# One chain of reciprocal roots per attention, dilated attention in three parts, gate rows one step later

## The chip, the cores and the metric

The kernel runs on one core of a Trainium2 chip. A core has a matrix engine (TensorE, PE in the profile; its weight loads are PEld), three engines for elementwise work (VectorE is DVE, ScalarE is ACT, GpSimd is POOL) and SyncE (SP), which issues most DMA transfers. Each engine executes its own instructions in order and waits on semaphores for the others. The metric is the device time of one execution in microseconds (us), which every time below is in. "Granted clock" is the share of full TensorE speed that the throttle granted in a stretch.

## The reference

One decoder layer for 256 tokens of width 2048, in float32. Three token mixers read the same normalised input and are gated, summed and projected; a SwiGLU block of width 5632 follows.

```python
def mixing_sublayer(h, w_in, ...):
    proj = h @ w_in                              # split by columns
    (q_sb, k_sb, v_sb, q_dil, k_dil, v_dil, q_gla, k_gla, v_gla, r_gla, a_gla, gate_cols) = ...
    qa, ka = rms_norm(heads(q_sb), gain), rms_norm(heads(k_sb), gain)     # 6 heads of 128
    o_sb = stick_breaking_attention(qa, ka, v_sb)
    qb, kb = rms_norm(heads(q_dil), gain), rms_norm(heads(k_dil), gain)   # 6 heads of 128
    o_dil = dilated_mixture(qb, kb, v_dil, slopes)
    o_g = gla_chunked(q_gla, k_gla, v_gla, log_a)                         # 4 heads
    o_gla = rms_norm(o_g, gain) * silu(r_gla)
    g = sigmoid(gate_cols.reshape(b, t, 3, d))
    y = g0 * (o_sb @ w_br_sb) + g1 * (o_dil @ w_br_dil) + g2 * (o_gla @ w_br_gla)
    return y @ w_out
# layer: mod = silu(c) @ w_ada + b_ada gives six vectors of 2048: shift1, scale1, gate1, shift2, scale2, gate2
x = x + gate1 * mixing_sublayer(rms_norm(x) * (1 + scale1) + shift1)
x = x + gate2 * swiglu(rms_norm(x) * (1 + scale2) + shift2)
```

`rms_norm` of a head multiplies it by the reciprocal root of the mean of its squares. The dilated mixture runs a softmax attention for each of three groups of two heads, and mixes the groups by the softmax of their log-denominators (lse).

## The kernel before

**Matmuls.** Each float32 weight matmul is done as three with rounded operands (`mm3`, L154 to L156): both operands are held as a high and a low part, and high*high, high*low and low*high are summed in PSUM. `load_weights` brings weights in pieces of 512 KB: a DMA into `raw`, issued from SP; a cast on ACT to `whi` (L148); a subtraction on DVE to `wlo` (L149), called "split" below. There are four buffers each of `whi` and `wlo`. A block is one product of 512 output columns for both halves of the tokens: with all 16 chunks of K it is 96 matmuls of 512 columns. It accumulates in banks named `acc` (four in PSUM); all else uses banks named `misc` (four too).

**Order.** A scheduler orders the instructions on each engine by program order, dependences and priorities. What stands in `prio()` (weight loads, casts, splits and the copies that empty a finished block) is moved ahead by 4000 places; `tc.issue_after(x)` holds an instruction back until x is issued. So small work written between two blocks in the program falls among the matmuls of the next blocks.

**Stages.** After the modulation vectors and the first norm, `proj_block` multiplies by the columns of q, k and v in four groups along K. In the last group come blocks 0 to 4, `stick_breaking()`, `gla()`, blocks 5 to 8, `dilated()`, then two blocks of r (stage "r"), then the gates: `gate_block(0, 0..2)` copies three finished blocks to `A` buffers, and one sigmoid over each of these three is issued later (L914); the gate blocks (1, 0..2) and further follow, with the sigmoid taken straight from PSUM. Behind them are the branch products, w_out, the second norm and the FFN.

**Norms of q and k.** `qk_norm(b, h0, h1, gain)` does one block of projections at a time: squares on ACT with a sum for each head and half of the tokens (L569); `rsqrt` on the 4 to 8 sums, which is one DVE operation, Ln and Exp on ACT (L242 and L243) and four small DVE operations ending with L248; a multiply on DVE for each half of the tokens (L574, up to four heads wide); transposes on PE, four into one bank (L581), and one eviction for each bank on ACT, which applies the gain (L582). Stick-breaking calls it for blocks 0, 1 and 2 (eight sums each), dilated attention for blocks 4 to 7 (24 sums in all).

**Dilated attention.** `dilated()` then multiplies scores for each head (L768, L769) into a bank, adds the bias on DVE, takes the exponential with its sum on ACT, forms lse and its softmax (a Ln, an Exp and small DVE operations, L781 to L792), the coefficients (L795 to L797), scales the probabilities (L806, 18 operations), transposes them (L810), copies them out of PSUM on ACT (L812) and multiplies by v (L813, L814). The result is split into the buffer OD.

**Modulation in the background.** Three modulation vectors (shift2, gate1, scale2) are summed on DVE while the mixers run (L257, L259): a DMA brings 512 KB of `w_ada` into a buffer of the ring `ring["tags"]`, and one DVE operation adds it up. `tick` advances this by `state["rate"]` steps (0.8, then 0.6 at the r blocks, 0.4 in the FFN) for every two chunks of K of a block. The gate vectors are then spread over all partitions by `rows_of`: for each 256 columns a cast and a split into the buffer T6 (L846, L847) and, one step later, two products with a matrix of ones (L850, L851). gate1 goes this way during the branch products, gate2 in the FFN.

Of the kernel before, what the change touches and what calls it, by code (L numbers as in the profile page):

```python
# [10 lines left out]
F32 = mybir.dt.float32  # L11
F32R = mybir.dt.float32r
U8 = mybir.dt.uint8
AF = mybir.ActivationFunctionType
ALU = mybir.AluOpType
AX = mybir.AxisListType

P = 128
T = 256
NT = T // P  # L20
D = 2048
KC = D // P
# [44 lines left out]
def trunk(ctx: ExitStack, tc: tile.TileContext, I, out):  # L67
# [21 lines left out]
    def scr(shape, dtype=F32):  # L89
        return sp.tile(shape, dtype, tag="scr", name=nm("scr"))  # L90
# [4 lines left out]
    def misc_bank(shape):  # L95
        return psm.tile(shape, F32, tag="misc", name=nm("misc"))
# [81 lines left out]
    ident = const.tile([P, P], F32, name="ident")  # L178
    make_identity(nc, ident)
    made = next(i for i in reversed(nc.cur_bb.bb.instructions) if i.engine == mybir.EngineType.Pool)  # L180
    ones = const.tile([P, P], F32, name="ones")
    nc.vector.memset(ones, 1.0)
    ones_r = const.tile([P, P], F32R, name="ones_r")
    nc.vector.tensor_copy(ones_r, ones)
    eps_c = const.tile([P, 2], F32, name="eps_c")
    nc.vector.memset(eps_c[:, 0:1], EPS)
    nc.vector.memset(eps_c[:, 1:2], 1.5)

# [369 lines left out]
    def head2(c):  # L558
        return A[c // 4][:, :, (c % 4) * P : (c % 4 + 1) * P]

    def qk_norm(b, h0, h1, gain):

        n = h1 - h0
        blk = A[b].rearrange("p t (h d) -> p t h d", d=P)
        ss = small([P, NT, n])
        for t in range(NT):
            for h in range(n):
                junk = scr([P, P])
                nc.scalar.activation(junk, blk[:, t, h0 + h, :], AF.Square, accum_out=ss[:, t, h : h + 1])  # L569
        r = rsqrt(ss.rearrange("p t h -> p (t h)"), 1.0 / P, [P, NT * n])  # L570
        r = r.rearrange("p (t h) -> p t h", t=NT)
        for t in range(NT):
            v = blk[:, t, h0:h1, :]
            nc.vector.tensor_tensor(  # L574
                v, v, r[:, t, :].unsqueeze(2).to_broadcast([P, n, P]), op=ALU.mult
            )
        for h in range(h0, h1, 2):
            ps = misc_bank([P, NT, 2, P])
            for t in range(NT):
                for i in range(2):  # L580
                    nc.tensor.transpose(ps[:, t, i, :], blk[:, t, h + i, :], ident)  # L581
            nc.scalar.activation(blk[:, :, h : h + 2, :], ps, AF.Copy, scale=gain(h))  # L582


    W3 = 3 * P
# [2 lines left out]
    def stick_breaking():  # L588
        os_ = [S(f"OS{j}", [P, 2, 2, T], F32R) for j in range(3)]
        hi = [o[:, 0] for o in os_]  # L590
        lo = [o[:, 1] for o in os_]
        qn = lambda h: qg_sb[:, 0:1]
        kn = lambda h: vec[:, ROW_SBK : ROW_SBK + 1]
        qk_norm(0, 0, 4, qn)
        qk_norm(1, 0, 4, lambda h: qn(h) if h < 2 else kn(h))
        qk_norm(2, 0, 4, kn)
        for h in range(N_SB):
            cq, ck, cv = h, N_SB + h, 2 * N_SB + h
            z = misc_bank([P, W3])
            nc.tensor.matmul(z[:, 0:T].rearrange("p (t d) -> p t d", t=NT), head(ck, 0), head2(cq), start=True, stop=True)  # L600
            nc.tensor.matmul(z[:, T:W3], head(ck, 1), head(cq, 1), start=True, stop=True)
            soft = scr([P, W3])
            nc.scalar.activation(soft, z, AF.Abs)
            nc.scalar.activation(soft, soft, AF.Exp, scale=-1.0)
            nc.scalar.activation(soft, soft, AF.Ln, bias=1.0)
            neg = scr([P, W3])
            nc.vector.scalar_tensor_tensor(neg, z, 0.0, soft, op0=ALU.max, op1=ALU.add)
            for d0 in (0, T):
                nc.vector.tensor_mul(neg[:, d0 : d0 + P], neg[:, d0 : d0 + P], causal)
            lb = soft  # L610
            nc.vector.scalar_tensor_tensor(lb, z, 0.0, soft, op0=ALU.min, op1=ALU.subtract)
            cum = misc_bank([P, W3])
            nc.tensor.matmul(cum, low, neg, start=True, stop=False)  # L613
            nc.tensor.matmul(cum[:, P:T], ones, neg[:, T:W3], start=False, stop=True)
            nc.vector.tensor_tensor(lb, lb, cum, op=ALU.subtract)
            w = neg
            nc.scalar.activation(w, lb, AF.Exp)
            for d0 in (0, T):
                nc.vector.tensor_mul(w[:, d0 : d0 + P], w[:, d0 : d0 + P], causal)
            o = misc_bank([P, T])  # L620
            nc.tensor.matmul(o, head(cv, 0), w[:, 0:T], start=True, stop=False)
            nc.tensor.matmul(o[:, P:T], head(cv, 1), w[:, T:W3], start=False, stop=True)
            split_from_psum(hi[h // 2][:, h % 2, :], lo[h // 2][:, h % 2, :], o)
        return hi, lo
# [125 lines left out]
        return og  # L750


    def dilated():
        qn = lambda h: qg_sb[:, 1:2]
        kn = lambda h: vec[:, ROW_DILK : ROW_DILK + 1]
        qk_norm(4, 2, 4, qn)
        qk_norm(5, 0, 4, qn)
        qk_norm(6, 0, 4, kn)
        qk_norm(7, 0, 2, kn)
        prob = [S(f"T{j}", [P, 2, W3]) for j in range(3)]  # L760
        mx = const.tile([P, NT, N_DIL], F32, name="dmax")
        sm = const.tile([P, NT, N_DIL], F32, name="dsum")
# [27 lines left out]
        den = small([P, NT, 2])  # L790
        nc.vector.tensor_add(den, G(lse, 0), G(lse, 1))
        nc.vector.tensor_add(den, den, G(lse, 2))  # L792
        coef = const.tile([P, NT, N_DIL], F32, name="dcoef")
        for g in range(3):
            nc.vector.tensor_mul(G(coef, g), G(sm, g), den)  # L795
# [3 lines left out]
        for j in range(2):  # L799
            o = misc_bank([P, T])  # L800
            for g in range(3):
                h = 2 * g + j
                cv = 30 + h
                p = prob[g][:, j, :]
                for t, (a, b) in enumerate(spans):
                    nc.vector.tensor_scalar(p[:, a:b], p[:, a:b], coef[:, t, h : h + 1], None, op0=ALU.mult)  # L806

                pt = misc_bank([P, W3])
                for i in range(3):
                    nc.tensor.transpose(pt[:, i * P : (i + 1) * P], p[:, i * P : (i + 1) * P], ident)  # L810
                pT = scr([P, W3])
                nc.scalar.copy(pT, pt)  # L812
                nc.tensor.matmul(o, head(cv, 0), pT[:, 0:T], start=g == 0, stop=False)  # L813
                nc.tensor.matmul(o[:, P:T], head(cv, 1), pT[:, T:W3], start=False, stop=g == 2)  # L814
            split_from_psum(oT[:, 0, j, :], oT[:, 1, j, :], o)
# [15 lines left out]
    def rows_of(name, seg, acc):  # L831

        quarters = [a[:, c : c + NB] for a in acc for c in (0, NB)]
        for j, q in enumerate(quarters):
            br = scr([1, NB])
            nc.sync.dma_start(br, I["b_ada"][:, seg * D + j * NB : seg * D + (j + 1) * NB])
            nc.vector.tensor_add(q[0:1, :], q[0:1, :], br)
            yield
        for _ in range(4):
            yield  # L840
        for q in quarters:
            ps = misc_bank([P, NB])
            for c in (slice(0, T), slice(T, NB)):
                hl = S("T6", [P, 2, T], F32R)
                hi, lo = hl[:, 0, :], hl[:, 1, :]
                nc.scalar.copy(hi, q[:, c])  # L846
                nc.vector.tensor_tensor(lo, q[:, c], hi.bitcast(F32), op=ALU.subtract)  # L847
                yield
                with tc.issue_after(state["mm"].ins):
                    nc.tensor.matmul(ps[:, c], ones_r, hi, start=True, stop=False)  # L850
                    nc.tensor.matmul(ps[:, c], ones_r, lo, start=False, stop=True)  # L851
            nc.scalar.copy(q, ps)
            yield
        state[name] = quarters
# [19 lines left out]
    og = gla()  # L874
    for b in range(5, 9):
        proj_block(LAST, b)
    od = dilated()

    state["rate"] = RATE_MID
    ring["tags"] = ("AR0", "AR1", "KC", "KD")  # L880

    rr = []
    for j in range(2):
        pss = [acc_bank() for _ in range(NT)]
        block(pss, h_at, w_in, 0, KC, (13 + j) * NB)
        r = S(f"A{j}", [P, NT, NB])
        with prio():
            for t in range(NT):
                nc.scalar.copy(r[:, t, :], pss[t])
        rr.append(r)  # L890

    gtags = (("A2", "A3", "A4"), ("A7", "A8", "T0"))
    gates = {}

    def gate_block(n, br):
        pss = [acc_bank() for _ in range(NT)]
        c0 = COL_G + br * D + n * NB
        block(pss, h_at, w_in, 0, KC, c0)
        g = S(gtags[n % 2][br], [P, NT, NB])
        with prio():  # L900
            for t in range(NT):
                if n == 0:
                    nc.scalar.copy(g[:, t, :], pss[t])
                else:
                    nc.scalar.activation(g[:, t, :], pss[t], AF.Sigmoid)
        gates[n, br] = g

    for br in range(3):
        gate_block(0, br)


# [264 lines left out]
```

## Time and profile before

| what | value |
|---|---|
| median of three runs | 1629.87 (1628.82 to 1631.06) |
| the profiled execution | 1630.8, of which span 1629.0 |
| granted TensorE clock, mean | 0.998 |
| matmuls | 7346 |
| first scores of stick-breaking (L600) | 276.1 |
| first transposes of dilated attention (L581 for blocks 4 to 7) | 460.7 |
| first products with v of dilated attention (L813) | 503.7 |
| row sums of gate1 and gate2 (L851) | 661.2 to 1289.4 |

The span runs from the first to the last recorded instruction of one execution; the profiled execution's own time adds what lies around it. The times in the last three rows are starts, counted from the span's start, which is also how rows of the timeline are given: start, duration, engine, line, operation, output<-input by buffer names, shapes, and the number of instructions that the row groups; brackets hold the engine's idle time before the row and what ended it. In a list of waits each line gives the instruction that waited, what it waited for, the total, the number of waits and the longest. A row of the windows view gives a stretch, its length, for each engine in the order PE, PEld, DVE, ACT, POOL its busy time with the number of instructions in brackets, then the granted clock, the busy share of DMA, and GB/s.

### The profile page before, as it was taken

The numbers are of one execution on the slowest core, as the hardware profiler recorded it, in microseconds if no ns is written. First come the engines' busy times: TensorE is split into PE (matmuls) and PEld (weight loads), VectorE is DVE, ScalarE is ACT, GpSimd is POOL, SyncE is SP. The second block draws the span as 40 slices with busy tenths as digits, with TensorE's granted clock in tenths as the row PEclk, the third lists the DMA queues.
The fourth block names the chain that finished last, engine by engine and source line by source line (L and its number), as shares of the span: only waits on it lengthen the run. The fifth ranks groups of instructions, "written<-read, shape, count | busy, mean of one in ns | idle before, by whom it ended". The sixth has DMA issues, their size and how long they took to land.

```text
span 1629.0 us, 19997 instructions
## 1 busy us (share of the span) xinstructions
PE 1608.1 (99%) x7346; PEld 1325.8 (81%) x7346; DVE 1121.9 (69%) x1322; ACT 801.5 (49%) x1130; POOL 5.3 (0%) x14
## 2 busy tenths in 40 slices
PE   8999999999999999999999999999999999999998
PEld 7878888788777888788887888888888888888887
DVE  6799996869688787877756566767655555454453
ACT  4654449764775444444446544444444444333332
POOL 1000000000000000000000000000000000000000
PEclk9999999999999999999999999999999999999999
DMA  9999996865777999988766478887666666666663
GB/s 319 339 333 325 329 312 201 287 224 167 230 225 247 308 310 312 306 278 303 258 192 209 147 236 262 273 269 257 211 192 182 191 187 189 192 205 194 205 207 109
DMA packets 194593, 395.94 MB, mean 243 GB/s; under 512 B 12914, under 2 KB 27928, under 8 KB 194496
## 3 DMA queue, kind: packets, MB, share of 16 engines
q1 hardware_dynamic: 194272, 394.67, 74.6%
q8 instruction: 57, 0.93, 0.2%
q14 instruction: 40, 0.33, 0.1%
q0 software_dynamic: 224, 0.01, 0.0%
HBM read 392.53 MB, written 2.10 MB: 242 GB/s over the span
## 4 chain that ended last, share of the span: by engine, by line
PE 88%; DMA 5%; DVE 3%; ACT 2%; issue 1%; SPq 0%; DVEq 0%; ACTq 0%
PE acc L156 28%; PE acc L154 28%; PE acc L155 27%; DMA raw<-w_in 2%; DMA raw<-w_br_gla 1%; ACT whi L148 1%; DMA A<-w_ada 1%; DVE wlo L149 1%; DMA KD<-w_ada 1%; PE misc L701 1%; PE misc L962 1%; DVE ada L259 1%; PE misc L308 0%; DMA raw<-w_ffn_in 0%; PE misc L613 0%
## 5 line engine op out<-in xcount | busy, mean ns | idle before, releaser
L149 DVE TENSOR_TENSOR wlo<-raw,whi 128x1024 fp32r<-128x1024 f32 (+1 forms) x546 | 651.8, 1198 | 431.4 <-ACT whi L148 429.5
L148 ACT CAST whi<-raw 128x1024 fp32r<-128x1024 f32 (+1 forms) x546 | 561.7, 1032 | 706.3 <-PE acc L156 561.8
L155 PE MATMUL acc<-wlo,H 128*128 128x512 f32 x1576 | 616.9, 391 | 1.0 <-DVE wlo L149 1.0
L154 PE MATMUL acc<-whi,H 128*128 128x512 f32 x1576 | 616.2, 392 | 0.5 <-ACT H L416 0.4
L156 PE MATMUL acc<-whi,H 128*128 128x512 f32 x1576 | 616.2, 391 | 0.4 <-DVE H L422 0.4
L156 PEld LDWEIGHTS acc<-whi,H 128*128 128x128 f32 x1576 | 296.4, 188 | 63.3 <-DVE H L422 1.5
L155 PEld LDWEIGHTS acc<-wlo,H 128*128 128x128 f32 x1576 | 296.6, 188 | 61.5 <-DVE wlo L149 1.4
L154 PEld LDWEIGHTS acc<-whi,H 128*128 128x128 f32 x1576 | 296.7, 188 | 61.3 <-ACT H L416 0.9
L155 PE MATMUL acc<-wlo,A 128*128 128x512 f32 x312 | 121.5, 390 | 0.6 <-DVE wlo L149 0.6
L154 PE MATMUL acc<-whi,A 128*128 128x512 f32 x312 | 121.9, 391 | 0.0
L156 PE MATMUL acc<-whi,A 128*128 128x512 f32 x280 | 109.1, 390 | 0.0
L259 DVE SCALAR_TENSOR_TENSOR ada<-AR,csil,ada 128x1024 f32<-128x1024 f32 x59 | 75.2, 1278 | 3.7 <-DMA AR<-w_ada 3.6
L155 PEld LDWEIGHTS acc<-wlo,A 128*128 128x128 f32 x312 | 58.6, 188 | 12.9 <-DVE wlo L149 1.0
L154 PEld LDWEIGHTS acc<-whi,A 128*128 128x128 f32 x312 | 58.6, 188 | 11.9
L156 PEld LDWEIGHTS acc<-whi,A 128*128 128x128 f32 x280 | 52.6, 188 | 11.1
L154 PE MATMUL acc<-whi,T 128*128 128x512 f32 x120 | 46.7, 389 | 0.0
L155 PE MATMUL acc<-wlo,T 128*128 128x512 f32 x120 | 46.7, 389 | 0.0
L156 PE MATMUL acc<-whi,T 128*128 128x512 f32 x120 | 46.7, 389 | 0.0
L156 PE MATMUL acc<-whi,OS 128*128 128x512 f32 x112 | 43.6, 390 | 0.0
L459 ACT COPY A<-acc 128x512 f32<-128x512 f32 x50 | 29.0, 585 | 17.6 <-PE acc L156 16.4
L259 DVE SCALAR_TENSOR_TENSOR ada<-OS,csil,ada 128x1024 f32<-128x1024 f32 (+2 forms) x33 | 35.6, 1078 | 1.1 <-DMA OS<-w_ada 0.9
L461 DVE TENSOR_TENSOR A<-A,acc 128x512 f32<-128x512 f32 x48 | 31.5, 682 | 2.0 <-PE acc L156 1.8
(334 smaller groups left out, 1227.9 us busy)
## 6 DMA issues: line engine op xcount, KB each, us to landing
raw<-w_in SPq DMA_DIRECT2D x205, 512.0 KB, 5.1
raw<-w_ffn_in SPq DMA_DIRECT2D x176, 512.0 KB, 3.9
raw<-w_ffn_out SPq DMA_DIRECT2D x88, 512.0 KB, 4.6
AR<-w_ada SPq DMA_DIRECT2D x79, 512.0 KB, 5.0
raw<-w_out SPq DMA_DIRECT2D x32, 512.0 KB, 4.4
KC<-w_ada SPq DMA_DIRECT2D x30, 512.0 KB, 5.5
KD<-w_ada SPq DMA_DIRECT2D x19, 512.0 KB, 5.6
OS<-w_ada SPq DMA_DIRECT2D x16, 512.0 KB, 6.7
```

What stands on the lines that cost most here:

```text
L148: state["cast"] = nc.scalar.copy(hi[:, :n, :], raw[:, :n, :])
L149: state["split"] = nc.vector.tensor_tensor(lo[:, :n, :], raw[:, :n, :], hi[:, :n, :].bitcast(F32), op=ALU.subtract)
L154: nc.tensor.matmul(ps, lh, rh, start=start, stop=False, skip_group_check=seeded)
L155: nc.tensor.matmul(ps, lh, rl, start=False, stop=False, skip_group_check=seeded)
L156: state["mm"] = nc.tensor.matmul(ps, ll, rh, start=False, stop=stop, skip_group_check=seeded)
L259: nc.vector.scalar_tensor_tensor(acc, raw, c, acc, op0=ALU.mult, op1=ALU.add)
L459: nc.scalar.copy(A[b][:, t, :], pss[t])
L461: nc.vector.tensor_add(A[b][:, t, :], A[b][:, t, :], pss[t])
L701: nc.tensor.matmul(ps[:n, h, L:], at(lhs, h, t)[:, :n], at(rhs, h, t)[:, L:], start=True, stop=True)
L962: nc.tensor.transpose(ps[:, i, :], src[:, i * P : (i + 1) * P], ident)
```

## The change

- **Norms**: `qk_norm(parts)` takes all blocks of an attention at once. It issues all squares, one `rsqrt` over 24 sums, and all multiplies. The transposes and evictions are in the new `qk_turn(parts, behind)`, which holds the transposes back behind an instruction if one is given. Stick-breaking calls the two in a row.
- **Dilated attention**: `qk_norm(dil_parts)` is called after projection block 8, where `dilated()` stood. `dilated()` now holds the transposes, scores and lse; it is called after r block 0, with its transposes behind the last matmul issued. The coefficients and all that follows are the new `mixture()`, called after `gate_block(0, 0)`, its transposes held back in the same way.
- **Ring**: its fourth buffer is OD instead of KD until `mixture()` is called, and KD from then on.
- **Gate rows**: one more step lies between a split and its two products in `rows_of`.
- **Ones**: the float32 tile of ones becomes a view of the rounded one, `ones_r`.

```diff
-    ones = const.tile([P, P], F32, name="ones")
-    nc.vector.memset(ones, 1.0)
+    eps_c = const.tile([P, 3], F32, name="eps_c")
+    nc.vector.memset(eps_c[:, 2:3], 1.0)
     ones_r = const.tile([P, P], F32R, name="ones_r")
-    nc.vector.tensor_copy(ones_r, ones)
-    eps_c = const.tile([P, 2], F32, name="eps_c")
+    nc.vector.tensor_copy(ones_r, eps_c[:, 2:3].to_broadcast([P, P]))
+    ones = ones_r.bitcast(F32)
...
-    def qk_norm(b, h0, h1, gain):
+    def qk_norm(parts):
-        n = h1 - h0
-        blk = A[b].rearrange("p t (h d) -> p t h d", d=P)
+        n = sum(h1 - h0 for _, h0, h1, _ in parts)
         ss = small([P, NT, n])
+        places, o = [], 0
+        for b, h0, h1, _ in parts:
+            for t in range(NT):
+                for h in range(h0, h1):
+                    junk = scr([P, P])
+                    i = o + h - h0
+                    nc.scalar.activation(junk, heads(b)[:, t, h, :], AF.Square, accum_out=ss[:, t, i : i + 1])
+            places.append(slice(o, o + h1 - h0))
+            o += h1 - h0
         r = rsqrt(ss.rearrange("p t h -> p (t h)"), 1.0 / P, [P, NT * n])
...
+        for (b, h0, h1, _), c in zip(parts, places):
+            for t in range(NT):
+                v = heads(b)[:, t, h0:h1, :]
+                nc.vector.tensor_tensor(
+                    v, v, r[:, t, c].unsqueeze(2).to_broadcast([P, h1 - h0, P]), op=ALU.mult
+                )
+
+    def qk_turn(parts, behind=None):
+        for b, h0, h1, gain in parts:
+            for h in range(h0, h1, 2):
+                ps = misc_bank([P, NT, 2, P])
+                for t in range(NT):
+                    for i in range(2):
+                        with tc.issue_after(behind) if behind is not None else nullcontext():
+                            nc.tensor.transpose(ps[:, t, i, :], heads(b)[:, t, h + i, :], ident)
+                nc.scalar.activation(heads(b)[:, :, h : h + 2, :], ps, AF.Copy, scale=gain(h))
...
-        qk_norm(0, 0, 4, qn)
-        qk_norm(1, 0, 4, lambda h: qn(h) if h < 2 else kn(h))
-        qk_norm(2, 0, 4, kn)
+        parts = ((0, 0, 4, qn), (1, 0, 4, lambda h: qn(h) if h < 2 else kn(h)), (2, 0, 4, kn))
+        qk_norm(parts)
+        qk_turn(parts)
...
+    dil_parts = ((4, 2, 4, dil_q), (5, 0, 4, dil_q), (6, 0, 4, dil_k), (7, 0, 2, dil_k))
     def dilated():
-        qk_norm(4, 2, 4, qn)
...
+        qk_turn(dil_parts, state["mm"].ins)
...
+        return prob, sm, lse, den, spans
+
+    def mixture(prob, sm, lse, den, spans):
+        G = lambda x, g: x[:, :, 2 * g : 2 * g + 2]
         coef = const.tile([P, NT, N_DIL], F32, name="dcoef")
...
-                    nc.tensor.transpose(pt[:, i * P : (i + 1) * P], p[:, i * P : (i + 1) * P], ident)
+                    with tc.issue_after(state["mm"].ins):
+                        nc.tensor.transpose(pt[:, i * P : (i + 1) * P], p[:, i * P : (i + 1) * P], ident)
... rows_of:
                 nc.vector.tensor_tensor(lo, q[:, c], hi.bitcast(F32), op=ALU.subtract)
                 yield
+                yield
                 with tc.issue_after(state["mm"].ins):
...
     for b in range(5, 9):
         proj_block(LAST, b)
-    od = dilated()
+    qk_norm(dil_parts)
     state["rate"] = RATE_MID
-    ring["tags"] = ("AR0", "AR1", "KC", "KD")
+    ring["tags"] = ("AR0", "AR1", "KC", "OD")
... for j in range(2):  (blocks of r)
         rr.append(r)
+        if j == 0:
+            groups = dilated()
...
-    for br in range(3):
+    gate_block(0, 0)
+    ring["tags"] = ("AR0", "AR1", "KC", "KD")
+    od = mixture(*groups)
+    for br in range(1, 3):
         gate_block(0, br)
```

More of the change, by code (lines that the diff above doesn't have):

```diff
@@ L559, in head2, with heads @@
         return A[c // 4][:, :, (c % 4) * P : (c % 4 + 1) * P]
-    def qk_norm(b, h0, h1, gain):
-        n = h1 - h0
-        blk = A[b].rearrange("p t (h d) -> p t h d", d=P)
+    def heads(b):
+        return A[b].rearrange("p t (h d) -> p t h d", d=P)
+    def qk_norm(parts):
+        n = sum(h1 - h0 for _, h0, h1, _ in parts)
         ss = small([P, NT, n])
[L566 to L569, printed above, removed]
+        places, o = [], 0
[7 more added lines that the diff above has]
+            o += h1 - h0
@@ L570, in qk_norm @@
         r = rsqrt(ss.rearrange("p t h -> p (t h)"), 1.0 / P, [P, NT * n])
         r = r.rearrange("p (t h) -> p t h", t=NT)
[L572 to L578, printed above, removed]
-            for t in range(NT):
-                for i in range(2):
-                    nc.tensor.transpose(ps[:, t, i, :], blk[:, t, h + i, :], ident)
-            nc.scalar.activation(blk[:, :, h : h + 2, :], ps, AF.Copy, scale=gain(h))
+        for (b, h0, h1, _), c in zip(parts, places):
+            for t in range(NT):
+                v = heads(b)[:, t, h0:h1, :]
+                nc.vector.tensor_tensor(
+                    v, v, r[:, t, c].unsqueeze(2).to_broadcast([P, h1 - h0, P]), op=ALU.mult
+                )
@@ L750, in gla @@
         return og
+    dil_q = lambda h: qg_sb[:, 1:2]
+    dil_k = lambda h: vec[:, ROW_DILK : ROW_DILK + 1]
+    dil_parts = ((4, 2, 4, dil_q), (5, 0, 4, dil_q), (6, 0, 4, dil_k), (7, 0, 2, dil_k))
     def dilated():
-        qn = lambda h: qg_sb[:, 1:2]
-        kn = lambda h: vec[:, ROW_DILK : ROW_DILK + 1]
-        qk_norm(4, 2, 4, qn)
-        qk_norm(5, 0, 4, qn)
-        qk_norm(6, 0, 4, kn)
-        qk_norm(7, 0, 2, kn)
+        qk_turn(dil_parts, state["mm"].ins)
         prob = [S(f"T{j}", [P, 2, W3]) for j in range(3)]
```

## The prediction

> **What bounds the kernel now.** I read the page's shares first, then the chain that ended last, then TensorE's list of waits, and last the timeline around each wait on that list that the diff touches.
>
> ```profile
> span 1629.0 us, 19997 instructions
> PE 1608.1 (99%) x7346; PEld 1325.8 (81%) x7346; DVE 1121.9 (69%) x1322; ACT 801.5 (49%) x1130; POOL 5.3 (0%) x14
> PE 88%; DMA 5%; DVE 3%; ACT 2%; issue 1%; SPq 0%; DVEq 0%; ACTq 0%
> PE misc L581 <- DVE A L574: 2.7, 1, 2.7
> PE misc L810 <- DVE T L806: 1.7, 1, 1.7
> PE misc L851 <- DVE T L847: 1.2, 1, 1.2
> PE misc L581 <- ACT A L582: 0.9, 1, 0.9
> PE misc L813 <- ACT scr L812: 0.8, 1, 0.8
> ```
>
> TensorE is busy 99% and carries 88% of the chain, so shortening work on DVE or ACT is worth nothing by itself; only the moments at which TensorE stands still can be won. The diff touches all five waits shown: the transposes of stick-breaking (0.9) and dilated attention (2.7), the dilated mixture (1.7 and 0.8), and the gate rows (1.2). The matmul count does not change. I therefore price the change wait by wait, from starts of successive TensorE rows, because ends are modelled. Its order on each engine I take from the instruction order of the built changed kernel.
>
> **Part 1, stick-breaking: one chain for 24 heads.** Here the change costs.
>
> ```profile
> 267.69 1.05 ACT L148 CAST whi<-raw 128x1024 fp32r<-128x1024 f32 x1 [1.34 <-DMA raw<-w_in]
> 268.65 0.20 ACT L242 ACTIVATE tiny<-tiny 128x8 f32<-128x8 f32 x1
> 271.53 0.17 DVE L248 TENSOR_TENSOR tiny<-tiny,tiny 128x8 f32<-128x8 f32 x1
> 271.62 0.69 DVE L149 TENSOR_TENSOR wlo<-raw,whi 128x512 fp32r<-128x512 f32 x1
> 272.22 1.29 DVE L574 TENSOR_TENSOR A<-A,tiny 128x512 f32<-128x512 f32 x2
> 269.94 0.39 PE L156 MATMUL acc<-whi,H 128*128 128x512 f32 x1
> 270.17 1.91 PE L581 MATMUL misc<-ident,A 128*128 128x128 f32 x16
> 271.83 0.48 PE L154 MATMUL acc<-whi,H 128*128 128x512 f32 x1
> 274.31 1.23 PE L581 MATMUL misc<-ident,A 128*128 128x128 f32 x8 [0.86 <-ACT A L582]
> 276.08 0.66 PE L600 MATMUL misc<-A,A 128*128 128x256 f32 x2
> ```
>
> A matmul costs 0.23 (269.94 to 270.17), a transpose 0.10 (16 between 270.17 and 271.83). Before, 16 transposes need only the first two blocks, whose chains were done long ago; only the third block's eight hang on the late chain: its Ln at 268.65 stands behind a cast that waited 1.34 for its weights, and its L248 ends at 271.7. In the changed order the one chain keeps just those two places, so all six multiplies start at 271.7. One takes 0.62 (272.22, two in 1.29); a 512-wide split stands behind the first and a full split (1.2, as at 440.72 below) behind the fourth, so they end near 272.3, 273.6, 274.2, 274.8, 276.6 and 277.2. TensorE's order becomes 4 transposes, 3 matmuls, 4 transposes, 1 matmul, 8 transposes, 6 matmuls, 8 transposes, scores. It stands from 270.17 to 272.4, then 0.1 to 0.2 at three later places, and starts the scores at 277.7. Before they started at 276.08 with one matmul fewer behind them, so 276.3. **Loss 1.4.** The six evictions on ACT stay ahead of need.
>
> **Part 2, dilated transposes and scores.** Here the change gains.
>
> ```profile
> 457.63 0.39 PE L156 MATMUL acc<-whi,H 128*128 128x512 f32 x1
> 460.68 0.66 PE L581 MATMUL misc<-ident,A 128*128 128x128 f32 x4 [2.66 <-DVE A L574]
> 458.35:461.76 3.41, 1.08 (x7) 1.00 (x8) 3.41 (x5) 1.03 (x2) 0.00 (x0) 1.00 0.76 249
> 461.76:465.17 3.41, 3.41 (x12) 2.73 (x11) 2.62 (x8) 1.70 (x3) 0.00 (x0) 0.50 0.95 302
> 499.31:502.72 3.41, 1.92 (x10) 1.50 (x10) 3.15 (x11) 0.45 (x1) 0.00 (x0) 1.00 0.95 339
> 438.48 1.27 ACT L903 COPY A<-acc 128x512 f32<-128x512 f32 x2 [0.27 <-PE acc L156]
> 438.96 0.39 PE L154 MATMUL acc<-whi,H 128*128 128x512 f32 x1
> 440.72 1.22 DVE L149 TENSOR_TENSOR wlo<-raw,whi 128x1024 fp32r<-128x1024 f32 x1 [0.22 <-ACT whi L148]
> 441.03 1.27 ACT L582 ACTIVATE A<-misc,qgains 128x512 f32<-128x512 f32 x2
> 445.06 1.28 ACT L914 ACT_TABLE_LOAD   x1
> 446.35 1.06 ACT L914 ACTIVATE A<-A 128x1024 f32<-128x1024 f32 x1
> ```
>
> Before, TensorE loses 3.05 - 0.23 = 2.8 at 460.68, and then a window of 3.41 at a granted clock of 0.50 (windows view, the second of the two rows of 458 to 465; the clock is the figure behind POOL's count), which costs half of it, 1.7. Sum 4.5. That window follows one in which TensorE worked 1.08 of 3.41; one with 1.92 (499.31) was followed by none here.
>
> After, all squares stand in ACT's queue ahead of the chain, with no table reload among them, and the chain itself ends about 2 before it is needed. What is late next is ACT: the multiplies stand on DVE behind the split at 440.72, whose cast waits for the copies of the finished gate block (438.48). So the first two (256 wide) end at 442.6; TensorE, 15 matmuls after 438.96, is there at 442.4. Then the changed ACT order puts the table load and sigmoid (1.28 + 1.06) and another cast ahead of the evictions, and the split of that cast ahead of the last three multiplies: those end at 446.3 to 447.0, TensorE gets there 0.1 to 0.3 earlier. The fourth score needs the PSUM bank of the last eviction, 449.65, since a cast stands before it: wait 0.8. The sixth needs a bank that DVE frees behind another split: 0.3. Waits in all: 0.2 + 0.25 + 0.3 + 0.8 + 0.3 = 1.8, none over 1. **Gain 4.5 - 1.8 = 2.7.** Bounds: 4.5 if nothing waits, 0 if one long wait comes back. The four or so ACT table loads that go cost nothing now and bring nothing: ACT is at 49%.
>
> **Part 3, the mixture.** It comes 79 matmuls behind the scores instead of 127 (17.9 us for 28.8).
>
> ```profile
> 493.46 1.05 ACT L903 COPY A<-acc 128x512 f32<-128x512 f32 x2
> 496.17 1.28 ACT L914 ACT_TABLE_LOAD   x1
> 500.37 2.12 DVE L806 TENSOR_SCALAR T<-T,dcoef 128x128 f32<-128x128 f32 x9
> 503.22 0.47 ACT L812 COPY scr<-misc 128x384 f32<-128x384 f32 x1
> 498.70 0.39 PE L156 MATMUL acc<-whi,H 128*128 128x512 f32 x1
> 500.80 0.30 PE L810 MATMUL misc<-ident,T 128*128 128x128 f32 x1 [1.71 <-DVE T L806]
> 502.55 0.40 PE L154 MATMUL acc<-whi,H 128*128 128x512 f32 x1
> 503.75 0.70 PE L813 MATMUL misc<-scr,A 128*128 128x256 f32 x2 [0.80 <-ACT scr L812]
> ```
>
> Before: 2.10 - 0.23 and 1.20 - 0.23, 2.8 in all. After, count from E, the end of the preceding block. The second exponential runs behind the cast that can start 12 matmuls before E: -2.7 + 1.05 + 1.28 + 0.2 = E - 0.2. The small DVE operations then follow without the background sums that stood between them before, some 1.4, and the first product (2.12 / 9) ends at E + 1.5; TensorE comes at 7 matmuls, E + 1.6: no wait. The first copy out of PSUM now stands on ACT behind copies (0.3 + 1.05), cast (1.05), table load (1.28), sigmoid (1.06), cast (1.05) and takes 0.47: E + 6.3, where TensorE is after 22 matmuls and 3 transposes, E + 5.3. Wait 1.0, and some 0.45 at the later copies. **Gain 2.8 - 1.45 = 1.4**, between 2.8 and below 0 if the exponential chain slips by over 3.
>
> **Part 4, gate rows.**
>
> ```profile
> 679.59 0.40 PE L156 MATMUL acc<-whi,A 128*128 128x512 f32 x1
> 681.22 0.39 PE L851 MATMUL misc<-T,ones_r 128*128 128x256 f32 x1 [1.24 <-DVE T L847]
> ```
>
> The wait costs 1.63 - 0.23 = 1.4. With one more step between split and sum, the changed order has 24 to 60 matmuls between row pairs, over 5 us, and each split on DVE well ahead: **gain 1.4**, not under 0.
>
> The rest is free: the `ones` tile becomes a view (one small DVE operation in the stretch that waits for the first loads), the last GLA products move a few matmuls with the same wait, and the ring's new buffer brings one 512 KB load ahead of some w_in loads near 240, covered by splits that run ahead of TensorE; uncovered I bound it by the 1.34 that the cast at 267.69 waited for its weights.
>
> **The sum.** +1.4 - 2.7 - 1.4 - 1.4 = -4.1. The profiled execution took 1630.8 (span 1629.0 and 1.8 around it), so 1626.7; it lies 0.9 over the median of 1629.87, so for the median 1625.8.
>
> **A rule against the trace.** The long wait in part 1 (2.2, with 1.2 to 1.9 of a window's 3.41 worked, by where the window falls) lies between the 1.08 that was followed by half clock and the 1.92 that was not. So a half-clock window there, 1.7, is open. The Trainium skill, "TensorE: Matmul & The Clock Gate", section "HAM oscillation", says that the clock falls only after gaps over about 3.4 us; by it, part 1 would pay no half clock and the sum would stay at -4.1. The trace does not agree: 2.66 idle was enough at 460.68.
>
> **Rivals.**
> - *Half clock at stick-breaking*: as just priced, 1625.8 + 1.7 = 1627.5. For it: the long wait; against: it depends on a window's phase. Chance 0.13.
> - *All waits go*: the weights before the chain land 1.3 earlier, the matmuls run on, the turn is free: -1.4 - 1.8 more, 1622.6. Against it: the places in the queues. Chance 0.16.
> - *The dilated wait only moves*: copies, cast, table load and sigmoid on ACT hold the evictions so long that a wait over 2.3 with its half clock returns; gain 0 in part 2, 1628.5. For it: ACT's order; against: the longest single wait that I find there is 0.8. Chance 0.14.
> - *Slower*: five background sums of w_ada stand on DVE between the splits and the tail of the dilated chain, and others before the exponential's tail. DVE works in order; if such a sum's load lands more than two splits' lead late (5.4, 24 matmuls), split and multiply wait behind it, TensorE idles some 2.7 and pays 1.7 of half clock. At both places: 8.8 - 4.1, so 1634.6. For it: the SP order mixes these loads with w_in anew; against: such waits are short now (below). Chance 0.15.
>
> ```profile
> L259 DVE SCALAR_TENSOR_TENSOR ada<-AR,csil,ada 128x1024 f32<-128x1024 f32 x59 | 75.2, 1278 | 3.7 <-DMA AR<-w_ada 3.6
> ```
>
> **Numbers.** 0.42 remain for the forecast, with 1.5 either way. About 0.2% (3.26 us) is what a measurement of this kernel can tell from no change: faster is under 1626.6, slower over 1633.1. Faster: 0.7 of the forecast (0.29), all of the second rival (0.16), a quarter of the first (0.03), a tenth of the third (0.01): 0.50. Slower: 0.85 of the last and a little of the third: 0.13. The rest, 0.37, is the same. The range 1622.4 to 1631.0 takes in all but the last rival and the tails.
>
> **What would show it.** Right: TensorE's list of waits has the stick-breaking transposes first, about 2.2, waiting for DVE; the dilated transposes show waits under 1 and no clock of 0.50 near 460; the first matmul on the mixture's copies waits about 1 for ACT; no wait at the gate rows. Wrong: a wait over 2.3 at the dilated transposes or scores, DVE's L149 or L259 waiting for w_ada there, or stick-breaking without its wait.

## The result

The changed kernel took 1622.27 us (median of five runs, 1620.65 to 1624.61) against 1629.87 (five runs): a ratio of 0.9959, 95% interval 0.9948 to 0.9970, so 7.6 us less, between 4.9 and 8.5. A second set of six runs of it gave 1620.90; the median of all eleven is 1621.83. The forecast was 1625.8, 4.1 less. The direction was right; the size was about half of what came. The measured time is 3.5 under the forecast, whose own spread was 1.5 either way, and 0.1 below the lower end of the range (1622.4).

The profile after, its page first (span, busy time of each engine, and the shares of the chain that ended last):

```profile
span 1620.5 us, 19955 instructions
PE 1604.7 (99%) x7346; PEld 1324.8 (82%) x7346; DVE 1117.9 (69%) x1297; ACT 795.2 (49%) x1116; POOL 5.3 (0%) x14
PE 92%; DMA 3%; DVE 2%; ACT 2%; issue 1%; SPq 0%; DVEq 0%; ACTq 0%
```

TensorE has as many matmuls as before and is still the bound; its share of the chain rose from 88% to 92%. Of the five waits in the list of before that the change touches, TensorE's list of waits has these left (in total, times, longest):

```profile
PE misc L594 <- DVE A L582: 1.9, 1, 1.9
PE misc L827 <- DVE T L822: 0.8, 1, 0.8
```

L594 are the transposes of the two norms (L581 before), L827 those of the mixture (L810 before). The 1.9 is stick-breaking's; dilated attention has no entry left, nor have the evictions, the copies of the mixture and the gate rows. GLA's wait for ACT (L742 before, 0.8) is gone too.

To see where the time went I took, for each matmul, the time to the next start less the usual time for its kind, and summed it over stretches of as many matmuls in both traces. In each pair the kernel before comes first, then the changed one: the first 200 matmuls 7.4 and 6.3; stick-breaking's transposes and first scores 2.6 and 5.3; the end of GLA 3.8 and 2.6; the stretch with dilated attention and mixture 11.8 and 5.2; the branch products 1.0 and 0.5; the gate1 rows 1.7 and 0.1. The differences add up to 8.3 of the 8.5 by which the spans differ.

**Stick-breaking** (timeline, then the windows view: length, busy time of PE, PEld, DVE, ACT, POOL, granted clock, DMA share, GB/s):

```profile
267.51 0.22 ACT L242 ACTIVATE tiny<-tiny 128x24 f32<-128x24 f32 x1
270.44 0.18 DVE L248 TENSOR_TENSOR tiny<-tiny,tiny 128x24 f32<-128x24 f32 x1
271.49 0.63 PE L594 MATMUL misc<-ident,A 128*128 128x128 f32 x4 [1.93 <-DVE A L582]
269.40:272.86 3.46, 1.53 (x10) 1.14 (x10) 3.43 (x6) 3.07 (x6) 0.00 (x0) 0.99 0.72 195
272.86:276.27 3.41, 3.41 (x15) 3.12 (x14) 3.23 (x5) 2.21 (x4) 0.00 (x0) 0.51 0.78 198
```

The one chain ends at 270.6 with the last of its small operations; only then does the first multiply run, and TensorE has stood 1.93 for it. Before, the first 16 transposes didn't need that chain. In the window of that stand it worked 1.53 of 3.46, and the next window ran at half clock. The forecast had the wait at 2.2, and the half clock as a rival.

**Dilated attention**:

```profile
442.00 2.56 DVE L582 TENSOR_TENSOR A<-A,tiny 128x256 f32<-128x256 f32 x5
442.50 0.76 PE L594 MATMUL misc<-ident,A 128*128 128x128 f32 x4
448.92 0.70 ACT L595 ACTIVATE A<-misc,vec 128x512 f32<-128x512 f32 x1
449.64 0.38 PE L780 MATMUL misc<-A,A 128*128 128x128 f32 x2
```

The multiplies start at 442.0 and TensorE arrives at 442.5 without a wait. The last eviction ends at 449.62, and the fourth score starts at 449.64; the forecast had TensorE there at 448.85, waiting 0.8.

**Mixture**:

```profile
467.87 0.21 ACT L801 ACTIVATE tiny<-tiny 128x12 f32<-128x12 f32 x1
470.15 0.75 DVE L822 TENSOR_SCALAR T<-T,dcoef 128x128 f32<-128x128 f32 x3
470.58 0.30 PE L827 MATMUL misc<-ident,T 128*128 128x128 f32 x1 [0.81 <-DVE T L822]
473.26 0.47 ACT L829 COPY scr<-misc 128x384 f32<-128x384 f32 x1
474.38 0.59 PE L830 MATMUL misc<-scr,A 128*128 128x256 f32 x2
```

The first product waits 0.81 (the forecast had no wait there), and the first copy is done at 473.73, ahead of TensorE at 474.38 (the forecast had a wait of 1.0).

### The profile page after: what moved, and what is told of

Its sections match the earlier page's. It is cut to its first block, busy times and chain, and to the rows that moved or that the text cites. A ratio compares the mean times of both kernels' runs of the same rounds, so it can differ in the third digit from the quotient of the medians.

```text
span 1620.5 us, 19955 instructions
## 1 busy us (share of the span) xinstructions
PE 1604.7 (99%) x7346; PEld 1324.8 (82%) x7346; DVE 1117.9 (69%) x1297; ACT 795.2 (49%) x1116; POOL 5.3 (0%) x14
## 4 chain that ended last, share of the span: by engine, by line
PE 92%; DMA 3%; DVE 2%; ACT 2%; issue 1%; SPq 0%; DVEq 0%; ACTq 0%
PE acc L156 29%; PE acc L154 29%; PE acc L155 29%; DVE wlo L149 1%; DMA A<-w_ada 1%; DMA raw<-w_in 1%; ACT whi L148 1%; DMA raw<-w_br_gla 1%; PE misc L714 1%; PE misc L985 1%; PE misc L594 0%; PE misc L308 0%; PE misc L626 0%; DMA raw<-w_br_sb 0%; PE misc L756 0%
## 5 line engine op out<-in xcount | busy, mean ns | idle before, releaser
L259 DVE SCALAR_TENSOR_TENSOR ada<-OS,csil,ada 128x1024 f32<-128x1024 f32 (+2 forms) x33 | 35.6, 1079 | 1.5 <-DMA OS<-w_ada 1.2
```

Of the source, the lines that this page charges most:

```text
L259: nc.vector.scalar_tensor_tensor(acc, raw, c, acc, op0=ALU.mult, op1=ALU.add)
```

## The experiments

The forecast's parts fall into five edits: one chain at stick-breaking, one chain at dilated attention, its three places, the ring's buffer, the gate rows. I took them out of the changed kernel or put them alone into the kernel before. The kernel before, run beside them, took 1629.28, 1629.62 and 1629.47 in the three groups (21, 21 and 17 runs).

**1. Stick-breaking's norms apart, in the changed kernel.**

```diff
-        qk_norm(parts)
-        qk_turn(parts)
+        for p in parts:
+            qk_norm((p,))
+            qk_turn((p,))
```

> The changed kernel with stick-breaking's norms again one block at a time (three chains of eight sums), all else as changed. Theory A (the one chain costs what the profile of the changed kernel shows there: TensorE stands 1.9 before the transposes and works the next 3.41 at half clock, together some 2.7 more than before): 1622.3 - 2.7 = 1619.6, no wait over 1 at those transposes, no clock of 0.50 near 272. Theory B (the loss there is repaid later, because weights run further ahead after it): no difference, 1622.3.

Measured: 1619.78, ratio to before 0.9940 (0.9926 to 0.9953). It is 2.5 below the changed kernel's first five runs, 1.1 below its second six. The wait left at those transposes (TensorE's list of waits):

```profile
PE misc L594 <- ACT A L595: 0.5, 1, 0.5
```

By the rows this is theory A. By the time it is theory A against the first five runs of the changed kernel; the intervals of this run and of the second six (0.9938 to 0.9963, run 11) overlap. All five executions here are shorter than nine of the eleven of the changed kernel.

**2. One chain at stick-breaking alone, in the kernel before** (all other parts as before).

> The kernel before with the one chain of stick-breaking alone (and the view for the ones). Theory A (the chain's price belongs to it, whatever follows): 1629.9 + 2.7 = 1632.6, with a wait of some 1.9 at the transposes and a clock of 0.50 behind it; 1631.3 if the wait comes without the half clock. Theory B (repaid later): 1629.9.

Measured: 1629.46 over eleven runs, ratio 1.0001 (0.9992 to 1.0010). The timeline at the transposes and the windows behind them:

```profile
270.91 0.63 PE L594 MATMUL misc<-ident,A 128*128 128x128 f32 x4 [2.08 <-DVE A L582]
269.98:273.39 3.41, 2.48 (x17) 2.07 (x18) 3.38 (x7) 2.91 (x6) 0.00 (x0) 1.00 0.79 237
273.39:276.80 3.41, 3.41 (x23) 2.90 (x23) 2.12 (x3) 2.34 (x5) 0.00 (x0) 1.00 0.74 220
```

The wait is there, 2.08, but no half clock: the window of the first transposes holds 2.48 of work. So 2.7 was no fixed price. The interval leaves at most 1.6 for it, which takes in the 1.4 of the forecast only near its end, and also zero; in this profile the branch products and the gate rows lost 1.3 less than in the profile of before, for which I have no cause. Theory B is neither shown nor excluded.

**3. Without the gate rows' step, in the changed kernel** (`yield` once instead of twice).

> The changed kernel without the added step in the gate rows. Theory A (the step hides the split): 1622.3 + 1.5 = 1623.8, and TensorE waits some 1.2 for a split once at the row sums. Theory B (the wait of before was an accident of where the rows fell among the other work, which the rest of the change moves): 1622.3, no such wait.

Measured: 1623.78, ratio 0.9961 (0.9948 to 0.9973), so 1.5 more than the changed kernel's first set and 2.9 more than its second; the ratios' intervals overlap. TensorE's list of waits has the split again:

```profile
PE misc L868 <- DVE T L864: 1.1, 1, 1.1
```

Theory A by this wait; the time fits it, and would not decide alone.

**4. A ring of three, in the changed kernel.**

```diff
-    ring["tags"] = ("AR0", "AR1", "KC", "OD")
+    ring["tags"] = ("AR0", "AR1", "KC")
```

> The changed kernel with a ring of three buffers (without OD) until the mixture. Theory A (the wait of 1.0 for ACT at GLA's products, near 420 in the kernel before, hangs on a background sum whose load of w_ada had no free buffer; OD is what removed it): the sum waits some 1.0 for its load again and TensorE 1.0 at the products, 1623.3; a little more if other sums come late at the dilated part. Theory B (that wait went because the norms of dilated attention no longer share ACT and DVE with GLA): no wait there, 1622.3.

Measured: 1625.05 over eleven runs, ratio 0.9975 (0.9966 to 0.9984): 2.8 more than the changed kernel's first set, 4.2 more than its second. The profiled execution is the slowest of the eleven (1629.59), so its rows show the mechanism and not its size:

```profile
419.21 1.28 DVE L259 SCALAR_TENSOR_TENSOR ada<-AR,csil,ada 128x1024 f32<-128x1024 f32 x1 [1.84 <-DMA AR<-w_ada]
PE misc L755 <- ACT scr L758: 1.1, 2, 0.9
455.00 0.44 PE L594 MATMUL misc<-ident,A 128*128 128x128 f32 x2 [1.87 <-DVE A L582]
456.36:459.77 3.41, 3.41 (x13) 2.78 (x11) 3.41 (x7) 1.53 (x3) 0.00 (x0) 0.50 0.61 183
```

A background sum waits 1.84 for its load, GLA's products wait for ACT again (L755 is L742 of before), and the dilated transposes wait 1.87 with a half clock behind them. One buffer, which the forecast had as free, carries a third to a half of the gain. Theory A, and more than it said. Without the buffer the order on TensorE changes too: the dilated transposes stand 1585 to 1594 weight matmuls from the start, in the changed kernel 1551 to 1559.

**5. One chain for dilated attention alone, in the kernel before.** `dilated()` stays in one piece at its old place:

```diff
-        qk_norm(4, 2, 4, qn)   # and three more
+        qk_norm(dil_parts)
+        qk_turn(dil_parts)
```

> The kernel before with one chain of 24 sums for dilated attention, in its old place and in one piece (and the view for the ones); no other part of the change. Theory A (the one chain is what removes the wait of 2.8 at the transposes and the half clock behind it: no table reloads between chains, all multiplies together): 1629.3 - 4.5 = 1624.8, up to 1626.6 where the half clock did not fall in each run; no wait over 1 at the transposes. Theory B (the later place of the transposes removes it): the wait stays, 1629.3.

Measured: 1627.49, ratio 0.9987 (0.9978 to 0.9996). Theory A for the transposes (longest wait there 0.9), but its time was not reached: the loss moved on to the mixture.

```profile
481.64 1.05 ACT L148 CAST whi<-raw 128x1024 fp32r<-128x1024 f32 x1 [4.61 <-DMA raw<-w_in]
491.04 1.22 DVE L259 SCALAR_TENSOR_TENSOR T<-AR,csil,T 128x1024 f32<-128x1024 f32 x1
492.80 0.32 PE L824 MATMUL misc<-ident,T 128*128 128x128 f32 x1 [2.81 <-DVE T L820]
492.96:496.37 3.41, 3.41 (x11) 2.65 (x11) 3.41 (x11) 0.48 (x1) 0.00 (x0) 0.50 0.88 300
```

The exponential ahead of the mixture stands on ACT behind a cast that waited 4.61 for its weights, five background sums stand between the small DVE operations behind it (the last at 491.04), and TensorE waits 2.81 and pays a half clock. The ring here is still that of before, with KD.

**6. The three places and the ring, but a chain for each part** (stick-breaking apart as in 1).

```diff
-    qk_norm(dil_parts)
+    for p in dil_parts:
+        qk_norm((p,))
```

> The changed kernel with separate chains in both attentions: stick-breaking as in the run before with its norms apart (1619.8), and dilated attention in its three new places but with one chain for each of its four parts. Theory A (the one chain removes the dilated wait): the last chains come late, the wait of 2 to 3 at the transposes or scores is back, 1622 to 1624. Theory B (the place removes it): 1619.8.

Measured: 1620.60, ratio 0.9951 (0.9938 to 0.9963), 0.8 over the 1619.78 of run 1 with overlapping runs (1620.21 to 1623.76 and 1618.59 to 1620.53). Nearer to theory B: with the places and the ring, the one chain adds little.

**7. The mixture behind gate block (0, 2), in the kernel of run 1.** The ring's switch to KD moves with it.

> The changed kernel with stick-breaking's norms apart (1619.8) and the mixture called behind gate block (0, 2) instead of behind (0, 0). Theory A (what lost 2.8 at the mixture before was that background sums stand between the small DVE operations ahead of its first products, and the copies behind casts on ACT; calling it early in the program puts these operations ahead): the waits return, 1619.8 + 2 to 3 = 1621.8 to 1622.8. Theory B (the longer ring, with its loads no longer late, is what freed DVE there): 1619.8.

Measured: 1619.56, ratio 0.9941 (0.9928 to 0.9953), as run 1; TensorE's list has no wait at the mixture at all. Theory B: an early call of the mixture is not what helped.

**8. The gate rows' step alone, in the kernel before.**

> The kernel before with only the added step in the gate rows. Theory A (it hides the split wherever the rest stands): 1629.3 - 1.5 = 1627.8, no wait for a split at the row sums. Theory B (without the other parts the rows fall otherwise, and a part of it is hidden or shifts elsewhere): 1629.3. Its first 50 us are those of the kernel before: if the half clock at 35 in that profile came with the tile of ones, it is here too, otherwise not.

Measured: 1627.97, ratio 0.9990 (0.9981 to 0.9998), 1.65 less, and no wait for a split at the row sums. Theory A. Its profile has no half clock at 35, with the tile of ones; run 5 has one (0.50 from 35.6), with the view. So the half clock at 35, and with it the 1.1 that the first 200 matmuls lost more in the profile of before, does not come from the ones; about one of the 8.5 between the two spans is no gain of the change. This profile holds one more thing: TensorE waits 2.7 at the dilated transposes, as in the profile of before, and pays no half clock there, since the wait is split between two windows (timeline row, then windows):

```profile
460.23 0.66 PE L581 MATMUL misc<-ident,A 128*128 128x128 f32 x4 [2.65 <-DVE A L574]
455.91:459.32 3.41, 1.67 (x8) 1.05 (x6) 2.25 (x3) 3.00 (x4) 0.00 (x0) 1.00 0.84 267
459.32:462.74 3.42, 2.51 (x15) 2.21 (x16) 3.41 (x7) 0.43 (x1) 0.00 (x0) 1.00 0.84 249
```

**9. The ring alone, in the kernel before.** OD is the ring's fourth buffer, and the dilated result goes to KD:

```diff
-        oT = S("OD", [P, 2, 2, T], F32R)
+        oT = S("KD", [P, 2, 2, T], F32R)
-    ring["tags"] = ("AR0", "AR1", "KC", "KD")
+    ring["tags"] = ("AR0", "AR1", "KC", "OD")
```

> The kernel before with only the ring changed: its fourth buffer is OD, and the result of dilated attention goes to KD instead (the branch weights that are kept in OD at the end of w_out go to KD too). Theory A (the ring's fourth buffer, which in the kernel before can't be loaded until the scores of dilated attention have read KD, makes the background sums late, and these hold up GLA's and the mixture's operations on DVE): the wait of 1.0 at GLA and part or all of the 2.8 at the mixture go, the dilated transposes keep theirs; 1629.5 - 2 to 3.8 = 1625.7 to 1627.5. Theory B (the place of the three parts did it): 1629.5.

Measured: 1627.81 over twelve runs, ratio 0.9991 (0.9981 to 1.0001); 1.7 less, with zero just inside. TensorE's list of waits:

```profile
PE misc L581 <- DVE A L574: 3.4, 2, 2.6
PE misc L810 <- DVE T L806: 1.5, 1, 1.5
```

GLA's wait and the mixture's wait for its copies are gone, the dilated transposes keep theirs. In direction theory A; by the time alone it isn't certain.

**10. Two chains at stick-breaking, in the changed kernel** (blocks 0 and 1 together, block 2 by itself).

> The changed kernel with two chains at stick-breaking: one for blocks 0 and 1 (16 sums), one for block 2 (8 sums). Theory A (the loss comes from tying the first blocks' multiplies to the last block's sums): as with the norms apart, 1619.8, no wait over 1 at the transposes. Theory B (a chain of more sums or multiplies close together is what costs): 1621 to 1622.3.

Measured: 1620.64. The timeline has theory A's side, 16 transposes in a row without a wait, and 0.28 at block 2:

```profile
270.35 1.91 PE L594 MATMUL misc<-ident,A 128*128 128x128 f32 x16
273.92 1.23 PE L594 MATMUL misc<-ident,A 128*128 128x128 f32 x8 [0.28 <-ACT A L595]
```

But beside it the changed kernel took 1620.90, so by the time the theories are not told apart. In this profile a later step of stick-breaking waits longer, the product behind the scores:

```profile
PE misc L627 <- DVE scr L623: 1.6, 2, 1.2
```

That wait is 0.2 in run 1. In the changed kernel (there L626) it is 0.2 in the first profile and 1.7 in that of run 11, so it differs between executions of one kernel and doesn't tell two chains from one.

**11. The changed kernel again.**

> The changed kernel once more, beside the others of this call: 1622.3 by every theory. Its profile is a second draw of where the half-clock windows fall: with a wait of 1.9 at stick-breaking again, a half clock behind it if more than half of a window passes without work, otherwise none and a time lower by 1.7 in that profile.

Measured: 1620.90. Its profiled execution waits less at stick-breaking and has no half clock there:

```profile
269.88 0.63 PE L594 MATMUL misc<-ident,A 128*128 128x128 f32 x4 [0.86 <-DVE A L582]
269.20:272.60 3.40, 2.72 (x20) 2.29 (x21) 3.40 (x6) 3.40 (x6) 0.00 (x0) 1.00 0.82 247
```

The wait of 1.9 is thus not a constant of the kernel; in the five profiles with one chain at stick-breaking (runs 2, 3, 4, 11 and the first of the changed kernel) TensorE waited there between 0.9 and 2.2, and the half clock followed in two.

**12. Ring and one dilated chain, in one piece, in the kernel before** (runs 5 and 9 together).

> The kernel before with the ring's fourth buffer OD (dilated result in KD) and one chain for dilated attention, called in one piece at the old place; stick-breaking and gate rows as before. Theory A (ring and chain are the gain; splitting the call into three parts adds nothing, since the scheduler then places transposes and mixture by itself at the same matmuls as in the changed kernel): 1619.8 with 1.5 more for the gate rows, 1621.3. Theory B (the three parts are needed): as with the one chain alone, 1627.5, less up to 1.0 for GLA.

Measured: 1622.08, ratio 0.9959 (0.9946 to 0.9972): 7.4 less, where the two alone took off 2.1 and 1.7. The row sums wait 1.6 for a split, as the step of the gate rows is missing here. The one wait left at dilated attention and mixture:

```profile
467.94 0.30 PE L824 MATMUL misc<-ident,T 128*128 128x128 f32 x1 [0.81 <-DVE T L820]
```

It is the wait of the changed kernel, 0.81. In the built kernels, counted in weight matmuls from the start, the dilated transposes of run 5 stand at 1585 to 1594 and the mixture's at 1730; in run 9 they stand at 1494 to 1627 and 1695; with both edits at 1551 to 1559 and 1639, exactly where the changed kernel has them. Theory A: the scheduler gives the same order without the split into three calls, and the time shows nothing that the split adds to these two edits (1621.3 lies in the interval, 1626.5 doesn't). Run 6 is the other side: with the split and the ring, the one chain is hardly needed.

## Why the prediction came out as it did

**What failed: the ring.** The forecast put the new buffer among the free things, with a cost of up to 1.34. Without it the changed kernel loses 2.8 to 4.2 (run 4). The rows that I should have read are these, of the kernel before: GLA's wait, the sum that waits, loads into the ring, the last read of KD by the scores, and, from the list of waits of 440 to 510, the wait of SyncE's queue before the first load into KD.

```profile
PE misc L742 <- ACT scr L745: 0.8, 1, 0.8
412.59 1.28 DVE L259 SCALAR_TENSOR_TENSOR ada<-AR,csil,ada 128x1024 f32<-128x1024 f32 x1 [1.01 <-DMA AR<-w_ada]
413.91 0.33 SPq L345 DMA_DIRECT2D AR<-w_ada  x1
431.12 0.34 SPq L345 DMA_DIRECT2D KC<-w_ada  x1
472.42 0.54 DVE L771 SCALAR_TENSOR_TENSOR T<-KD,misc 128x384 f32<-128x384 f32 x1
472.99 0.34 SPq L345 DMA_DIRECT2D KD<-w_ada  x1
SPq L345 <- DVE dmax L774: 7.1, 1, 7.1
```

KD holds the distances that the scores add (L771), so its first load can start only at 472.99; SyncE's queue stood 7.1 for it, until DVE had gone on to L774. Until then the ring is short of a buffer: between 400 and 470 it starts 11 loads, in the kernel after 17, where OD takes its turn at once:

```profile
413.54 1.28 DVE L259 SCALAR_TENSOR_TENSOR ada<-OD,csil,ada 128x1024 f32<-128x1024 f32 x1
414.84 0.33 SPq L345 DMA_DIRECT2D OD<-w_ada  x1
435.59 0.33 SPq L345 DMA_DIRECT2D OD<-w_ada  x1
```

The sums there wait for no load, and GLA's products no longer wait (1.0 between starts, which the forecast kept as "the same wait"; it returns in run 4). That the sum alone held them up is not shown. The chain of small DVE operations behind it ends no earlier in the changed kernel:

```profile
414.19 0.16 DVE L248 TENSOR_TENSOR tiny<-tiny,tiny 128x2 f32<-128x2 f32 x1
416.20 0.16 DVE L248 TENSOR_TENSOR tiny<-tiny,tiny 128x2 f32<-128x2 f32 x1
```

The first row is the kernel before, 6.6 behind its first product of L743 (407.63); the second the changed one, 6.5 behind the same product there (L756, 409.67). What differs is the order: with the buffer, ACT does both copies and a cast ahead of this chain's next step, and the last two groups of GLA's products stand at 1455 and 1465 weight matmuls instead of 1462 and 1477, in run 9 (the ring alone) as in the changed kernel.

The rest of the ring's gain fits the order too, though no run changes the order by itself: with the one chain, the ring brings scores and mixture 65 and 113 matmuls forward (1625 and 1752 before; 1595 and 1684 in run 4, without the buffer). The weights are also in time: between 440 and 510 ACT's casts wait 4.3 for `w_in` in the kernel before and 6.6 in run 5, 0.4 in run 9, and not at all in the changed kernel. The rows fit loads of `w_ada` that were put off and then stand among those of the weights: 10 start between 470 and 500 before, 5 after.

By the stretches above, stick-breaking lost 2.7 (1.4 forecast), dilated attention and mixture gained 6.6 (4.1 forecast), the end of GLA 1.2 (nothing forecast) and the gate1 rows 1.6 (1.4 forecast).

**Part 1** had the wait right (1.9 for 2.2) and, by run 1, the sign. Its size is between 1.1 and 2.5 by run 1 against the two sets of the changed kernel, at most 1.6 by run 2, which leaves zero open; 1.4 stands within the first and near the end of the second. The rival's half clock came in two of five profiles.

**Part 2** named the right losses, 2.8 and the 1.7 of half clock, and both went; but the 1.7 is not paid in every execution of the kernel's old order (run 8). The term that failed is the 1.8 of new waits: the list has none there. I had TensorE 0.8 too early at the fourth score (448.85 for 449.64). The cause that I gave, the one chain alone, was half of it: run 5 shows that it clears the transposes and that the mixture then pays; run 6 shows that places and ring do nearly the same without it.

**Part 3**: the gain was forecast as 1.4 with two waits of 1.0 and 0.45 left for ACT's copies. The trace has neither, and a wait of 0.8 for DVE instead, so about 2 of the 2.8 went. That it came from an earlier call is refuted (run 7).

**Part 4** was right: 1.4 forecast, 1.65 measured in run 8 and 1.5 or more in run 3, with the wait gone and back as forecast.

**Rivals.** "All waits go" gave 1622.6, next to the result, but by another way, so that is luck: its ground was weights that land earlier, while in fact waits went that I had priced and one that I had taken as unchanged. The rival on the slower side had sums of w_ada late on DVE; such late sums are there (1.01 in the kernel before, 1.84 in run 4), and the change removes them.

**What stays open:** what stick-breaking's one chain costs in the kernel before (run 2), what two chains there are worth in time (run 10), how much of the ring's gain is order and how much weights in time, and half clocks near 35, below.

## What to carry to other kernels

A buffer that is handed to a background ring while a foreground step still reads it is no buffer; find the first load into each in the trace before pricing a change of the ring. Edits that a scheduler orders are not additive (2.1 and 1.7 alone, 7.4 together), so compare the order of the built kernels with each edit alone before giving each its own sum. And one chain for all blocks is as late as the last block: it can pay where nothing waits for the first one (dilated attention, run 5), and makes TensorE wait where the first blocks' work stands next on it (stick-breaking, 0.9 to 2.2).

## What the runs showed of the hardware

A stand of less than 2 was enough for half clock, where it fell into one window of 3.41. After the first 50 us, eight windows in these profiles that came right before a half-clock window had between 0.65 (run 5) and 1.55 (run 4) of TensorE work; windows with 1.67 (run 8), 1.81 (run 3, from 268.41), 1.92 (before), 2.48 (run 2) and 2.72 (run 11) had none behind them. In the changed kernel the wait behind 1.53 was 1.93, while 2.65 in run 8, split between two windows, cost no clock. The Trainium skill, "TensorE: Matmul & The Clock Gate", section "HAM oscillation", asks for gaps over some 3.4; these runs disagree, as the 2.66 of the prediction did.

The half clock near 35 in the profiles of before and of run 5 does not fit this: the windows ahead of it hold 2.97 and 2.76 of work. In the profile of before, 1.39 of the 2.97 are products of one column each:

```profile
31.68 1.39 PE L300 MATMUL misc<-ones,ada 128*128 128x1 f32 x12
```

Whether such products count less as work for the clock, no run here tests.
